# Six gate products beside the banded attention, thirteen beside the sparse one, and the compression's temporaries in two other tiles

## The chip, the cores and the metric

The kernel runs on one NeuronCore of a Trainium2 chip. The metric is the device time of one execution in microseconds (us), from the first instruction to the last; lower is better. The engines are named as the profile names them: PE (TensorE, matrix products), PEld (its weight loads), DVE (VectorE), ACT (ScalarE), POOL (GpSimd) and SP (the queue that issues most transfers). Every engine runs its own list of instructions in order; semaphores tie them together.

## What is computed

The reference is a small model on 512 tokens of width 1024: one block with two feed-forward nets around a mixture of two attentions, then a second block of two layers. All is float32. What the change touches is the attention part of each of these two layers:

```python
g = sigmoid(h @ w_branch_gate)                 # 1024 -> 3 x 1024
o_a = nsa_attention(...)    # sparse: compressed, selected and windowed keys, 8 heads
o_b = swa_sink_attention(...)                  # banded: window of 128, 8 heads
o_c = mla_attention(...)                       # latent: low-rank queries and keys, 8 heads
merged = g_a * (o_a @ w_branch_a) + g_b * (o_b @ w_branch_b) + g_c * (o_c @ w_branch_c)
x = x + merged @ w_out
# inside nsa_attention, for keys and for values:
k_cmp = gelu(blocks(kc) @ w1) @ w2             # the compression
```

## The kernel before, in words

The activations stand with features on the partitions and 512 tokens along the row. A float32 product is made of three products of rounded parts, each part a high and a low piece: high by high, high by low, low by high. A **dense product** of this kind, 128 output features from 1024 inputs, is thus 24 matmuls of 128x512 (lines 143 to 145, `gemm`). Its weights come by a transfer into `wraw` and are taken apart by ACT (line 88, `whi`) and DVE (line 89, `wlo`), one instruction of 128x1024 each per product. A **gate product** is such a product out of `w_branch_gate`; there are 24 in a layer, and each also has a scaling on DVE (line 470), a tanh on ACT (line 471), both on a tile `gt`, and a transfer of `gt` to memory.

In `mix2` the attentions of a layer run one after the other: the banded one (`swa`, four pairs of heads), the sparse one (`nsa`, eight heads), the latent one (`mla`, eight heads). Each is a generator that gives up control after a head (the banded one after each first head of a pair and after each pair). At every such point `pump` lets other generators write a step: queries `qa`, `qb`, keys `kva`, the compression (`inp` prepares its input, `cmp_` has four steps, `end` takes its results), the latents `lt` (four dense products with their normalisation, then a small one), the gates `gts` and the output branches `brs`. A tuple such as `(qa, 1, gts, 1)` says which generators write how many steps. This fixes the order in which the work is written; a scheduler then orders each engine's list by a simulated timeline, and so may draw instructions forward past others that wait, as far as buffers allow.

Two sets of buffers matter for that. In this part all dense products share the two PSUM banks `ps_mm` (`narrow()`): a third product can't start before the first one's result has been taken out. And `mla` begins with four products (lines 1453 to 1455), each worth a quarter of a dense product; their results are taken out by ACT (line 91) and DVE (line 92) into tiles `v`, of which there are four. The compression's inputs (`FL`) hold two of them until it is done; the values of the sparse attention (`VS`) hold the other two until the last sparse head is done.

One sparse head is, on PE: `ps_s` products of keys and queries (line 969, with a mask by line 971), transposes of the probabilities into `ps_t` (995), products with the values into `ps_o` (1002, 1003), and the compressed branch (1280, 1294, 1300), together 98 matmuls, of 8 rows of scores each. Each row goes from PE to DVE (maximum, 973), ACT (exponent, 974), DVE (975, 990), ACT and DVE (halves `ph`, 98 and 99), PE (transposes), ACT (copies `pp`, 997 and 998) and back to PE. In the banded attention the matching lines are 1339 to 1344 (scores), 105 (transposes `ps_t`), 835 (copy `p`) and 1379 (`ps_o`).

The compression keeps two temporaries, `hT` and `s`, in tiles `gt`, of which there are two; the gates use the same two.

Of the kernel before, what the change touches and what calls it, by code (L numbers as in the profile page):

```python
# [844 lines left out]
class Block2(Block1):  # L845
# [205 lines left out]
    def mix2(self, X, U, a, i):  # L1051
# [50 lines left out]
        def queries(out, first):  # L1102
            for c0 in (first, first + 256):
                for ps in proj(c0, 256):
                    out.extend(self.stack_q(self.rope(ps, cosr, sinr), 0.125))
                    yield

        def keys_a():
            for c0 in (768, 1024):
                ka.append(self.stack_k(self.rope(next(proj(c0)), cosr, sinr)))  # L1110
                yield

        def keys_b():
            kb.append(self.stack_k(self.rope(next(proj(1816)), cosr, sinr)))
            yield
            kb.append(self.values_b(next(proj(1944)), R))
            yield

        def gates():
            nonlocal gd  # L1120
            for gd in self.gates(a["w_branch_gate_2"][i], uh, ul, R, 24, f"gates2_{i}"):
                yield

        def branches():
            yield from self.branch(gd[8:16], a["w_branch_b_2"][i], OB, ("uh", "uh"), merged, "ul")
            yield from self.branch(gd[0:8], a["w_branch_a_2"][i], OA, ("uh", "uh"), merged, "ul")


        kvb, kva, qb, qa = keys_b(), keys_a(), queries(QB, 1304), queries(QA, 0)
# [3 lines left out]
        inp, cmp_ = self.compress_in(FL, i, proj, cosr, sinr, R, flat), self.compress(a, i, flat)  # L1133
        gts, brs, lt = gates(), branches(), self.latents(a, i, proj, w_in, uh, ul, R, lat)
        KC = VC = None

        def last():
            nonlocal KC, VC
            KC, VC = next(cmp_)
            yield  # L1140
        end = last()
        plan = ((qb, 1, kva, 1), (inp, 1, qb, 1), (inp, 1, cmp_, 1), (qb, 1, cmp_, 1), (qa, 1, cmp_, 1), (qa, 1, cmp_, 1),
                (qa, 1, end, 1, gts, 1), (kva, 1, qa, 1, gts, 1))
        for n, _ in enumerate(self.swa(QB, *kb, i, OB)):
            self.pump(*plan[n])
        KS, KW = ka


        plan = ((lt, 2), (lt, 2, gts, 1), (lt, 1, gts, 2)) + ((gts, 3),) * 5
        for h, _ in enumerate(self.nsa(QA, KS, KW, KC, VS, VC, G, OA)):  # L1150
            self.pump(*plan[h])
        for h, _ in enumerate(self.mla(lat, a, i, OC)):
# [69 lines left out]
    def compress(self, a, i, flat):  # L1222

        nc = self.nc
        out = []
        for kv in range(2):
            w1 = a["a_cmp_w1_v_2" if kv else "a_cmp_w1_k_2"][i]
            hT, s = self.t("gt"), self.t("gt")
            w2 = a["a_cmp_w2_v_2" if kv else "a_cmp_w2_k_2"][i].rearrange("(k p) n -> p k n", p=128)
            w = hT[:, 128:384].rearrange("p (k n) -> p k n", k=2)  # L1230
            nc.sync.dma_start(w[:, :, 0:64], w2)
            if kv == 0:
                nc.sync.dma_start(w[:, :, 64:128], w2)

            ps = self.bank()
            for half in range(2):
                r = self.raw(8, 256)
                nc.sync.dma_start(r, w1[1024 * half:1024 * half + 1024].rearrange("(k p) n -> p k n", p=128))
                for j in range(8):
                    e = j % 2  # L1240
                    nc.tensor.matmul(ps[64 * e:64 * e + 64, 0:256], flat[kv][:, 8 * half + j].rearrange("p g n -> p (g n)"),
                                     r[:, j], start=half == 0 and j < 2, stop=half == 1 and j > 5)
            nc.scalar.activation(s[0:64, 0:256], ps[64:128, 0:256], AF.Copy)
            nc.vector.tensor_tensor(s[0:64, 0:256], ps[0:64, 0:256], s[0:64, 0:256], op=OP.add)
            yield
            ps = self.bank()
            for m in range(2):
                nc.tensor.transpose(ps[:, 64 * m:64 * m + 64], s[0:64, 128 * m:128 * m + 128], self.ident[0:64, 0:64])
            nc.scalar.activation(hT[:, 0:128], ps[:, 0:128], AF.Gelu_apprx_tanh)
            yield  # L1250
            if kv == 0:
                both = self.t("kc", F32R)
                ps = self.bank()
                for k in range(2):
                    nc.tensor.matmul(ps[:, 0:64], w[:, k], hT[:, 64 * k:64 * k + 64], start=k == 0, stop=k == 1)
                c = both[:, 0:128].rearrange("p (g e n) -> p e g n", g=2, e=2)
                self.split(c[:, 0], c[:, 1], ps[:, 0:64].rearrange("p (g n) -> p g n", g=2))
                out.append([c[:, :, g] for g in range(2)])
            else:
                c = both[:, 128:384]  # L1260
                for g in range(2):
                    ps = self.bank()
                    for k in range(2):
                        nc.tensor.matmul(ps[0:32, 0:64], hT[:, 64 * k + 32 * g:64 * k + 32 * g + 32], w[:, k, 0:64],
                                         start=k == 0, stop=k == 1)
                    o = 128 * g
                    for r in (0, 32):
                        self.split(c[r:r + 32, o:o + 64], c[r:r + 32, o + 64:o + 128], ps[0:32, 0:64], 1 / UP)
                out.append([c[0:64, 0:128], c[0:64, 128:256]])
        yield out  # L1270
# [334 lines left out]
```

## Time and profile before

| | us |
|---|---|
| median of 3 runs | 3258.23 |
| lowest and highest | 3254.02, 3265.27 |
| the profiled execution | 3259.47 |
| its span, first to last instruction | 3257.7 |
| PE busy in the span | 3171.5 (97%) |
| DVE, ACT, POOL busy | 1905.7, 1480.2, 350.7 |
| mean granted clock of PE | 0.985 |

The granted clock is 1.00 at 2.4 GHz and 0.50 at 1.2 GHz; a mean of 0.94 over a stretch says that 12% of it ran at the lower level, and that 6% of its length in PE's work was lost. The banded attention of the first layer lies at about 1265 to 1390 us, the sparse one overlaps its end and goes to 1620, the latent one to 1740; in the second layer they lie some 1005 us later. A matmul's end is modelled in the profile, so PE can show as busy while short waits lie between the starts of its matmuls.

### The profile page before, as it was taken

What the parts mean: (1) busy time and instruction counts of PE and PEld (TensorE: products, weight loads), DVE (VectorE), ACT (ScalarE), POOL (GpSimd) and SP (SyncE); (2) the same over time, 40 slices, a digit from 0 to 9 for tenths busy, and PEclk for the clock granted to TensorE, in tenths of its full rate; (3) what the DMA queues carried; (4) which work ended last, traced back from release to release, by engine and by line L of the source; (5) the groups of instructions that cost most, each with busy time, mean ns of one, the idle gap of its engine ahead of it and who ended that gap; (6) DMA issues with size and microseconds to landing.
All of it is one profiled execution on the core that took longest, in us unless ns stands there. A gap on an engine that the chain in (4) does not pass through costs nothing.

```text
span 3257.7 us, 44744 instructions
## 1 busy us (share of the span) xinstructions
PE 3171.5 (97%) x16695; PEld 2610.2 (80%) x16695; DVE 1905.7 (58%) x3745; ACT 1480.2 (45%) x2929; POOL 350.7 (11%) x562
## 2 busy tenths in 40 slices
PE   8999899999999998999999999999999999999998
PEld 7888888778888887778777888888778878788887
DVE  5344555555744458776677544357876677544355
ACT  4323335644432335667775322234766776322233
POOL 2200231102650020000003000000000002000001
PEclk9999999999999998999999999999989999999999
DMA  5432253336132325423265323224532246332322
GB/s 147 127 104 94 88 172 114 88 118 202 57 120 91 107 70 147 137 79 102 84 188 173 113 92 104 91 91 136 156 90 95 89 141 200 126 104 91 104 84 71
DMA packets 365737, 373.39 MB, mean 115 GB/s; under 512 B 48640, under 2 KB 317824, under 8 KB 365520
## 3 DMA queue, kind: packets, MB, share of 16 engines
q1 hardware_dynamic: 358672, 358.48, 35.5%
q0 software_dynamic: 6640, 12.01, 1.4%
q8 instruction: 131, 2.15, 0.3%
q14 instruction: 86, 0.70, 0.1%
q10 hardware_dynamic: 208, 0.05, 0.0%
HBM read 320.16 MB, written 44.91 MB: 112 GB/s over the span
## 4 chain that ended last, share of the span: by engine, by line
PE 91%; DVE 4%; DMA 2%; ACT 2%; issue 1%; SPq 0%; POOL 0%; DVEq 0%; ACTq 0%; POOLq 0%
PE ps_mm L143 13%; PE ps_mm L144 13%; PE ps_mm L145 13%; PE ps_s L145 6%; PE ps_s L143 6%; PE ps_s L144 6%; PE ps_t L143 6%; PE ps_t L145 6%; PE ps_t L144 6%; PE ps_s L969 3%; PE ps_t L995 2%; PE ps_o L1002 1%; PE ps_o L1003 1%; PE ps_t L105 1%; DMA gt<-gates 1%
## 5 line engine op out<-in xcount | busy, mean ns | idle before, releaser
L88 ACT ACTIVATE whi<-wraw 128x1024 fp32r<-128x1024 f32 (+4 forms) x422 | 414.7, 990 | 823.5 <-PE ps_mm L144 259.7
L143 PE MATMUL ps_mm<-uh,whi 128*128 128x512 f32 (+2 forms) x1648 | 647.0, 393 | 5.0 <-DVE ft L1041 2.8
L145 PE MATMUL ps_mm<-uh,wlo 128*128 128x512 f32 (+2 forms) x1648 | 644.2, 391 | 0.0
L144 PE MATMUL ps_mm<-ul,whi 128*128 128x512 f32 (+2 forms) x1520 | 593.6, 391 | 3.1 <-DVE ul L92 3.1
L89 DVE TENSOR_TENSOR wlo<-wraw,whi 128x1024 fp32r<-128x1024 f32 (+4 forms) x422 | 494.6, 1177 | 161.6 <-ACT whi L88 160.0
L143 PEld LDWEIGHTS ps_mm<-uh,whi 128*128 128x128 f32 (+1 forms) x1648 | 311.7, 189 | 65.9 <-DVE ft L1041 3.2
L145 PEld LDWEIGHTS ps_mm<-uh,wlo 128*128 128x128 f32 (+1 forms) x1648 | 311.0, 189 | 60.4 <-issue 0.2
L144 PEld LDWEIGHTS ps_mm<-ul,whi 128*128 128x128 f32 (+1 forms) x1520 | 287.2, 189 | 57.8 <-DVE ul L92 3.8
L143 PE MATMUL ps_t<-uh,whi 128*128 128x512 f32 (+1 forms) x600 | 231.2, 385 | 0.0
L145 PE MATMUL ps_t<-uh,wlo 128*128 128x512 f32 (+1 forms) x600 | 230.2, 384 | 0.0
L144 PE MATMUL ps_t<-ul,whi 128*128 128x512 f32 (+1 forms) x600 | 230.1, 383 | 0.0
L145 PE MATMUL ps_s<-uh,wlo 128*128 128x512 f32 (+1 forms) x544 | 208.6, 384 | 0.0
L144 PE MATMUL ps_s<-ul,whi 128*128 128x512 f32 (+1 forms) x544 | 208.6, 383 | 0.0
L143 PE MATMUL ps_s<-uh,whi 128*128 128x512 f32 (+1 forms) x544 | 208.4, 383 | 0.0
L88 ACT ACTIVATE dh<-wraw 128x768 fp32r<-128x768 f32 (+2 forms) x102 | 89.9, 898 | 209.1 <-PE ps_mm L144 68.8
L99 DVE SCALAR_TENSOR_TENSOR ph<-p,sa,ph 128x128 f16<-128x128 f32 (+2 forms) x224 | 124.6, 565 | 30.4 <-ACT ph L98 28.4
L89 DVE TENSOR_TENSOR dl<-wraw,dh 128x768 fp32r<-128x768 f32 (+2 forms) x102 | 105.1, 1044 | 62.6 <-ACT dh L88 62.2
L969 PE MATMUL ps_s<-k,q 128*128 128x256 f32 (+1 forms) x448 | 130.7, 383 | 2.4 <-ACT p L974 2.4
L144 PEld LDWEIGHTS ps_t<-ul,whi 128*128 128x128 f32 x600 | 114.8, 191 | 21.3
L143 PEld LDWEIGHTS ps_t<-uh,whi 128*128 128x128 f32 x600 | 114.7, 191 | 21.4
L145 PEld LDWEIGHTS ps_t<-uh,wlo 128*128 128x128 f32 x600 | 114.5, 191 | 21.6
L98 ACT ACTIVATE ph<-p,sa 128x128 f16<-128x128 f32 (+2 forms) x224 | 120.4, 554 | 25.0 <-DVE sa L990 18.7
(655 smaller groups left out, 6417.4 us busy)
## 6 DMA issues: line engine op xcount, KB each, us to landing
wraw<-w_in_in SPq DMA_DIRECT2D x28, 1024.0 KB, 5.4
wraw<-w_branch_gate_in SPq DMA_DIRECT2D x24, 1024.0 KB, 5.7
wraw<-ffn_w_gate_in SPq DMA_DIRECT2D x22, 1024.0 KB, 5.5
wraw<-ffn_w_up_in SPq DMA_DIRECT2D x22, 1024.0 KB, 5.4
wraw<-w_ffn_gate_in SPq DMA_DIRECT2D x22, 1024.0 KB, 5.9
wraw<-w_ffn_up_in SPq DMA_DIRECT2D x22, 1024.0 KB, 5.4
wraw<-ffn_w_down_in SPq DMA_DIRECT2D x24, 768.0 KB, 4.4
gates<-gt SPq DMA_DIRECT2D x64, 256.0 KB, 2.1
```

What stands on the lines that cost most here:

```text
L88: nc.scalar.activation(hi, src, AF.Copy)
L89: nc.vector.tensor_tensor(lo, src, hi.bitcast(F32), op=OP.subtract)
L98: self.nc.scalar.activation(h, P, AF.Copy, scale=scale)
L99: self.nc.vector.scalar_tensor_tensor(l, P, scale, h, op0=OP.mult, op1=OP.subtract)
L105: self.nc.tensor.matmul(out, hl[e][:, cols], self.ident16, start=e == 0, stop=e == 1)
L143: nc.tensor.matmul(o, w[0][k], xh[k][:, cols], start=k == 0, stop=False)
L144: nc.tensor.matmul(o, w[0][k], xl[k][:, cols], start=False, stop=False)
L145: nc.tensor.matmul(o, w[1][k], xh[k][:, cols], start=False, stop=k == kc - 1)
L969: nc.tensor.matmul(ps[:, 0:n], l, r, start=i == 0, stop=i == len(mms) - 1)
L995: nc.tensor.transpose(pt[:, e, k], hl[e][:, k * 128:k * 128 + 128], self.ident16)
L1002: nc.tensor.matmul(o, v, PH[:, k], start=first and k == 0, stop=False)
L1003: nc.tensor.matmul(o, v, PL[:, k], start=False, stop=last and k == nk - 1)
```

## The change

The tuples are altered. Beside the banded attention, `gts` now writes a step at each of the last six points instead of the last two. Beside the sparse one it writes none, none, one, two, three, two, three, two steps after heads 0 to 7, instead of none, one, two and five times three: 13 instead of 18. The rest of the 24 is written beside the latent attention: 5 instead of 4. The compression's `hT` goes from `gt` to a tile `c`, its `s` to a tile `ot`; of each there is one, which the sparse heads use later. No arithmetic is added or taken away.

```diff
         plan = ((qb, 1, kva, 1), (inp, 1, qb, 1), (inp, 1, cmp_, 1), (qb, 1, cmp_, 1), (qa, 1, cmp_, 1), (qa, 1, cmp_, 1),
-                (qa, 1, end, 1, gts, 1), (kva, 1, qa, 1, gts, 1))
+        plan = ((qb, 1, kva, 1), (inp, 1, qb, 1), (inp, 1, cmp_, 1, gts, 1), (qb, 1, cmp_, 1, gts, 1), (qa, 1, cmp_, 1, gts, 1),
+                (qa, 1, cmp_, 1, gts, 1), (qa, 1, end, 1, gts, 1), (kva, 1, qa, 1, gts, 1))
...
-        plan = ((lt, 2), (lt, 2, gts, 1), (lt, 1, gts, 2)) + ((gts, 3),) * 5
+        plan = ((lt, 2), (lt, 2), (lt, 1, gts, 1), (gts, 2), (gts, 3), (gts, 2), (gts, 3), (gts, 2))
...
-            hT, s = self.t("gt"), self.t("gt")
+            hT, s = self.t("c"), self.t("ot")
```

What the scheduler makes of it is seen in the engines' lists. First DVE in the banded attention of the first layer, around the first maximum of the fifth head (line 1348); `wlo` is a product's weights, `gt` the scaled result of a gate product, `rt` and `q` belong to the queries, the rest to the banded heads. Before:

```order
L99 SCALAR_TENSOR_TENSOR ph<-pp,sa,ph 128x128
L1348 TENSOR_REDUCE sa<-ps_s 128x1
L1349 TENSOR_REDUCE sa<-ps_s 128x1
L1358 TENSOR_TENSOR sa<-sa 128x4
L1351 TENSOR_SCALAR sa<-sa,sink 128x2
L1359 RECIPROCAL sa<-sa 128x4
L1360 TENSOR_SCALAR sa<-sa 128x4
```

After, up to the same maximum:

```order
L931 TENSOR_TENSOR rt<-rt,cs 128x512
L470 TENSOR_TENSOR gt<-ps_mm,r 128x512
L932 TENSOR_TENSOR rt<-rt,cs 128x512
L835 COPY p<-ps_t 128x256
L89 TENSOR_TENSOR wlo<-wraw,whi 128x1024
L1348 TENSOR_REDUCE sa<-ps_s 128x1
L1349 TENSOR_REDUCE sa<-ps_s 128x1
```

A gate product's result is now taken out among the banded heads; six stand ahead of the first sparse head's softmax (line 1283) where two stood.

Then ACT in the last sparse head of the first layer, from its compressed branch (`dr`) on; `whi` and `gt` belong to dense products. Before:

```order
L1287 ACTIVATE dr<-dr 128x128
L88 ACTIVATE whi<-wraw 128x1024
L98 ACTIVATE ph<-p,sa 128x512
L471 ACTIVATE gt<-gt 128x512
L974 ACTIVATE p,sa<-ps_s,sa 128x128
L974 ACTIVATE p,sa<-ps_s,sa 128x256
L98 ACTIVATE ph<-p,sa 128x128
L98 ACTIVATE ph<-p,sa 128x256
L88 ACTIVATE c<-ps_t 32x512
L88 ACTIVATE whi<-wraw 128x768
```

After:

```order
L1287 ACTIVATE dr<-dr 128x128
L974 ACTIVATE p,sa<-ps_s,sa 128x256
L98 ACTIVATE ph<-p,sa 128x128
L98 ACTIVATE ph<-p,sa 128x256
L997 ACTIVATE pp<-ps_t 128x4x128
L998 ACTIVATE pp<-ps_t 128x4x128
L974 ACTIVATE p,sa<-ps_s,sa 128x128
L88 ACTIVATE c<-ps_t 32x512
```

No weights and no gates are left in this head's list: they stand ahead of it.

Last PE in the same head, from two products of scores on; `ps_mm` is a dense product. Before:

```order
L969 MATMUL ps_s<-k,q 128x256 x2
L971 LDWEIGHTS identb
L971 MATMUL ps_s<-mask,identb 128x128
L969 MATMUL ps_s<-k,q 128x256
L145 MATMUL ps_mm<-uh,wlo 128x512
L143 MATMUL ps_mm<-uh,whi 128x512
L144 MATMUL ps_mm<-ul,whi 128x512
```

After:

```order
L969 MATMUL ps_s<-k,q 128x256 x2
L971 LDWEIGHTS identb
L971 MATMUL ps_s<-mask,identb 128x128
L969 MATMUL ps_s<-k,q 128x256
L1294 MATMUL ps_t<-ident,dr 32x128 x4
L1002 MATMUL ps_o<-pp,v 128x256
L1003 MATMUL ps_o<-pp,v 128x256
```

The dense matmuls that stood between this head's own are gone from it. Counted over PE's whole list, the longest run of matmuls without a dense one in the attention part is 61 in either layer before, and 163 in the first and 144 in the second after; both hold the whole last sparse head. The four products of lines 1453 to 1455 stand inside that head before, and ahead of the run after, in both layers.

## Rows read from the trace of the kernel before

**Rows 1.** The page: busy time of the engines, and the chain that ended last.
```profile
PE 3171.5 (97%) x16695; PEld 2610.2 (80%) x16695; DVE 1905.7 (58%) x3745; ACT 1480.2 (45%) x2929; POOL 350.7 (11%) x562
PE 91%; DVE 4%; DMA 2%; ACT 2%; issue 1%; SPq 0%; POOL 0%; DVEq 0%; ACTq 0%; POOLq 0%
```

**Rows 2.** Windows: stretch, length, busy us (instructions) per engine, clock, DMA share, GB/s.
```profile
1300.00:1360.00 60.00, 55.91 (x383) 42.63 (x383) 48.59 (x119) 43.41 (x108) 0.42 (x2) 0.94 0.50 153
1395.00:1440.00 45.00, 40.70 (x234) 32.31 (x234) 30.94 (x101) 31.25 (x79) 2.13 (x12) 0.85 0.20 63
1440.00:1600.00 160.00, 160.00 (x972) 128.79 (x971) 109.75 (x279) 111.55 (x273) 7.25 (x42) 1.00 0.29 92
1600.00:1640.00 40.00, 38.11 (x218) 30.14 (x217) 27.30 (x55) 27.99 (x62) 1.73 (x10) 1.00 0.31 90
2310.00:2360.00 50.00, 48.37 (x339) 35.66 (x334) 40.20 (x92) 36.72 (x92) 0.42 (x2) 1.00 0.52 157
2395.00:2450.00 55.00, 50.48 (x289) 40.78 (x288) 35.51 (x116) 35.00 (x91) 2.54 (x14) 0.81 0.17 53
2600.00:2640.00 40.00, 38.10 (x212) 30.41 (x211) 27.83 (x53) 26.89 (x57) 1.54 (x10) 1.00 0.34 96
```

**Rows 3.** Waits of PE, 1300 to 1360 us: us in total, times, longest.
```profile
PE ps_t L105 <- DVE ph L99: 2.8, 3, 1.3
PE ps_o L1379 <- DVE p L835: 0.8, 1, 0.8
```

**Rows 4.** Groups of instructions, 1440 to 1600 us: count, busy us, mean ns, idle before.
```profile
L143 PE MATMUL ps_mm<-uh,whi 128*128 128x512 f32 (+1 forms) x148 | 58.7, 397 | 0.0
...
L974 ACT ACTIVATE p<-ps_s,sa 128x128 f32<-128x128 f32 (+3 forms) x44 | 22.8, 521 | 9.6 <-DVE sa L973 7.9 <-DVE sa L975 1.6
L89 DVE TENSOR_TENSOR wlo<-wraw,whi 128x1024 fp32r<-128x1024 f32 (+1 forms) x18 | 21.7, 1207 | 1.4 <-ACT whi L88 1.2
...
L88 ACT ACTIVATE whi<-wraw 128x1024 fp32r<-128x1024 f32 (+1 forms) x18 | 18.9, 1052 | 7.4 <-PE ps_mm L144 7.4
...
L470 DVE TENSOR_TENSOR gt<-ps_mm,r 128x512 f32<-128x512 f32 x17 | 11.7, 686 | 3.8 <-PE ps_mm L145 3.8
L471 ACT ACTIVATE gt<-gt 128x512 f32<-128x512 f32 x17 | 10.8, 634 | 0.1
```

**Rows 5.** Timeline of PE, two dense matmuls: start us, us, what.
```profile
1281.41 0.39 PE L145 MATMUL ps_mm<-uh,wlo 128*128 128x512 f32 x1
...
1283.45 0.39 PE L145 MATMUL ps_mm<-uh,wlo 128*128 128x512 f32 x1
```

**Rows 6.** Windows: the four stretches of sparse heads without dense matmuls, and their sum.
```profile
1395.20:1405.70 10.50, 7.99 (x59) 5.91 (x58) 9.68 (x33) 9.24 (x25) 0.69 (x4) 0.98 0.03 4
1423.90:1437.90 14.00, 12.21 (x67) 9.58 (x67) 11.07 (x38) 10.94 (x28) 0.75 (x4) 0.69 0.34 113
2395.70:2409.20 13.50, 11.06 (x63) 8.14 (x61) 11.31 (x37) 10.36 (x29) 0.76 (x4) 0.73 0.03 4
2428.10:2442.40 14.30, 12.22 (x66) 9.50 (x66) 12.31 (x39) 11.54 (x30) 0.75 (x4) 0.66 0.33 110
sum 52.30, PE 43.48 PEld 33.13 DVE 44.37 ACT 42.09 POOL 2.95; mean PE 10.87 PEld 8.28 DVE 11.09 ACT 10.52 POOL 0.74
```

**Rows 7.** Timeline of ACT, first and last result `v` in the first layer.
```profile
1606.67 0.68 ACT L91 ACTIVATE v<-ps_mm,rv 128x512 fp32r<-128x512 f32 x1
...
1620.10 0.69 ACT L91 ACTIVATE v<-ps_mm,rv 128x512 fp32r<-128x512 f32 x1
```

**Rows 8.** Timeline of PE at the same place: idle us before, and releaser, in brackets.
```profile
1616.66 0.38 PE L1002 MATMUL ps_o<-pp,v 128*128 128x256 f32 x1 [1.23 <-ACT pp L997]
```

More of the change, by code (lines that the diff above doesn't have):

```diff
@@ L1141, in mix2 @@
         end = last()
-        plan = ((qb, 1, kva, 1), (inp, 1, qb, 1), (inp, 1, cmp_, 1), (qb, 1, cmp_, 1), (qa, 1, cmp_, 1), (qa, 1, cmp_, 1),
-                (qa, 1, end, 1, gts, 1), (kva, 1, qa, 1, gts, 1))
+        plan = ((qb, 1, kva, 1), (inp, 1, qb, 1), (inp, 1, cmp_, 1, gts, 1), (qb, 1, cmp_, 1, gts, 1), (qa, 1, cmp_, 1, gts, 1),
+                (qa, 1, cmp_, 1, gts, 1), (qa, 1, end, 1, gts, 1), (kva, 1, qa, 1, gts, 1))
         for n, _ in enumerate(self.swa(QB, *kb, i, OB)):
```

## The prediction

> **What bounds the kernel now.** I read the page's busy times and chain first. PE is busy for 97% of the span and carries 91% of the chain that ended last [rows 1]. The change adds and removes no matmul, so PE's work stays, and what can move is the time in which PE stands idle or runs at the lower clock. The windows by stage show where that is [rows 2]; there the reader compares PE's busy time with the length, and looks at the clock. Beside the banded attention of the first layer (1300 to 1360 us) PE is idle for 4.1 us and the mean clock is 0.94, which costs another 0.06 x 60 = 3.6 us; in the second layer (2310 to 2360) it is idle for 1.6 us at full clock. In the first sparse heads (1395 to 1440, 2395 to 2450) 4.3 and 4.5 us are idle and the clock costs 0.15 x 45 = 6.8 and 0.19 x 55 = 10.4 us, 26 us together. From 1440 to 1600 us, where sparse heads run with three dense products each, PE is never idle and the clock is 1.00. Last, I looked for what such a head costs without dense products [rows 6].
>
> **A gate product's price.** Nine dense matmuls start within 2.04 us [rows 5], 0.227 us each, so a product is 24 x 0.227 = 5.4 us of PE. It takes 1.2 + 0.7 = 1.9 us of DVE and 1.05 + 0.63 = 1.7 us of ACT [rows 4]. It is PE's filler: while it runs, DVE and ACT can finish the softmax that PE waits for.
>
> **What four more gate products gain beside the banded attention.** The waits named there are PE's transposes behind DVE's halves, and the value product behind a copy on DVE [rows 3]. DVE is busy for 48.6 of 60 us. Four products bring 22 us of work to PE and 7.6 us to DVE, so PE leads DVE by more than before, and the waits should shrink. At most all goes: 4.1 + 3.6 + 1.6 = 9.3 us over both layers. At least nothing goes, if the products stand behind the waits instead of in them. I take 7, since the order has gate results among the banded heads' rows and still keeps stretches of 52 to 66 matmuls without a dense one.
>
> **What the sparse heads lose.** The early heads look alike in the order: two stretches without dense matmuls in each layer, 53 and 61 (then 56 and 61) long before, 51 and 59 (62 and 56) after. I cost them at no change. The last head is another matter. Its own PE list holds 163 (first layer) and 144 matmuls (second) in a row without a dense one, 307 in all, or 307 / 98 = 3.13 heads. The reason lies in the buffers. Of mla's four first products two can be taken out early; the other two need the tiles of `VS`, which the last sparse head still reads. Now all four are issued ahead of that head, the last two hold both `ps_mm` banks through it, and no dense product can start. Before, this jam is short: the first of the four results is taken out at 1606.7 us, the last at 1620.1, and PE's visible wait in it is 1.2 us [rows 7, 8].
>
> Price from below: an unfilled head can't be faster than its busiest engine. From 1440 to 1600 us there are 44 rows of scores, 5.5 heads [rows 4]. ACT's 111.6 us less 18.9 for weights and 10.8 for gates is 81.9, or 14.9 us a head; DVE's 109.75 less 21.7 and 11.7 is 76.4, or 13.9. PE's 160 us less 3 x 148 x 0.227 = 101 is 59, or 10.8 us a head. Unfilled, a head thus loses at least 14.9 - 10.8 = 4.1 us, and 3.13 heads lose 12.8 us.
>
> Price from above: the four unfilled stretches have 255 matmuls in 52.3 us, 0.205 us each [rows 6], where the filled head pays 10.8 / 98 = 0.110. The 307 matmuls would take 62.9 instead of 33.8 us, a loss of 29.1. Those stretches also carry the latents' normalisation on DVE and ACT, which the last head doesn't, but like them it would run partly at the lower clock (0.66 to 0.98 there). I take the middle, 21 us, and keep 12.8 and 29.1 for the range. Of the present end of the sparse attention, idle for 1.9 us in each layer [rows 2], some 2.5 us together is replaced by this, not added to it.
>
> **The other edits.** The compression's temporaries move from `gt` to `c` and `ot`. Their order of reuse is the same (the second pass waits for the first), `c` and `ot` are next used by the first sparse head, after the compression, and the transfers of `w2` on SP wait for the same matmuls as before: nothing, covered by that order; if a gate had to wait for a `gt` instead, it would be one product of 5.4 us. One gate more beside the latent attention, where PE is full: nothing.
>
> **Sum.** 3259.5 (the profiled execution; the median is 1.2 lower) - 7 + 21 - 2.5 = 3271.0 us, of which the price of the unfilled heads alone spans 3262.8 to 3279.1. That is 0.4% slower. About 0.3%, 9.8 us, is what a measurement of this kernel can tell from no change.
>
> **A rule that says otherwise.** Rows 2 show a stretch where DVE is nearly full beside one where PE is. The Trainium skill, Perfetto Trace Analysis, Optimization Strategy, says that where the most contended engine changes over time, interleaving the regimes may improve performance; by that alone the sum would be 3259.5 - 9.3 = 3250 us. The same page says under that heading that bubbles on the engine that should be full can mean that there isn't enough PSUM for the next tile; by that the last head's loss stands, and the sum is mine. The trace bears out the first for 9.3 us in the banded part, and for the second shows only the short jam at 1616.7 us [rows 8]. The first rule's time is a part of the faster rival below and of its chance.
>
> **The rivals.**
> - *Only the engine limit.* The last heads cost the floor of 12.8 us and the banded part gives all 9.3: 3259.5 + 12.8 - 2.5 - 9.3 = 3260.5. For it: in the four stretches ACT is busy for 42.1 of 52.3 us and DVE for 44.4, near their limit, and part of that is the latents'. Against: a row's way from its scores to its values changes engine eight times.
> - *Dearer.* PE falls to the lower clock in the long run and stays there. Then a head takes 21.6 us of PE, more than ACT's 14.9, and 3.13 heads lose 33.8: 3259.5 + 33.8 - 2.5 - 7 = 3283.8. For it: three of the four stretches ran at 0.66 to 0.73 though they are a third as long.
> - *Faster: the filler is free where it was taken.* The last head finishes under PE's own pace because ACT and DVE are rid of the gates, so it costs nothing, and the banded part gives 9.3: 3250.2. If PE then also enters the first sparse heads without a gap and a quarter of their 26 us goes, it is 3259.5 - 9.3 - 6.5 = 3243.7. It decides from the point at which the last heads lose less than 6 us. Against: ACT's 14.9 us a head is above PE's 10.8 without any gate.
> - *The plan changes nothing,* because the scheduler undoes it: 3259.5. The order speaks against it: six gate results stand ahead of the first sparse softmax instead of two.
>
> **How the numbers follow.** My forecast 0.49 (its own times 3263 to 3279), the engine limit 0.22, dearer 0.17, faster 0.10, nothing 0.02. Slower by over 0.3% (above 3268) is the dearer case and 0.40 of the forecast: 0.57. Faster by over 0.3% (below 3248.5) is 0.08 of the faster case. The rest, 0.35, is within 0.3%. For 8 in 10 I leave out the faster case and the upper half of the dearer one: 3255 to 3285.
>
> **What would show it.** In the profile after: in each layer a stretch of some 25 to 35 us at the end of the sparse attention without `ps_mm` matmuls, with ACT and DVE at 80% or more, PE's idle time released by ACT and DVE lines 974 to 998, and a clock below 1.00; no such rows in the middle heads. The first and second `v` results should be taken out well ahead of the third and fourth, a whole head apart. Beside the banded attention idle time and lower clock should fall from 9.3 to 2 us or so. I am wrong if that last stretch loses under 6 us or over 34, if the stretches of the first sparse heads change by more than 5 us in either layer, or if the middle heads, now with two to three gates, show idle time of PE.

## The result and the profile after

The changed kernel takes 3285.61 us (median of 5 runs, 3277.22 to 3290.05), the kernel before 3260.00 in the same comparison (3254.02 to 3265.27). The ratio is 1.0071, with a 95% interval of 1.0047 to 1.0095: slower by 0.7%. The profiled execution of the changed kernel took 3285.61 us itself.

The page, as in [rows 1]:

```profile
PE 3179.7 (97%) x16695; PEld 2614.0 (80%) x16695; DVE 1905.1 (58%) x3745; ACT 1482.4 (45%) x2929; POOL 353.6 (11%) x562
PE 88%; DVE 5%; DMA 3%; ACT 2%; issue 1%; SPq 0%; POOL 0%; DVEq 0%; ACTq 0%; POOLq 0%
```

The engines' work is the same; PE holds 88% instead of 91% of the chain that ended last, and DVE and DMA have a point more each. The windows of the stages, as in [rows 2] (stretch, length, busy us per engine, clock):

```profile
1300.00:1360.00 60.00, 56.36 (x347) 43.55 (x347) 37.64 (x79) 34.52 (x75) 0.21 (x1) 0.97 0.47 145
1440.00:1574.00 134.00, 132.31 (x789) 106.69 (x788) 92.92 (x240) 93.13 (x228) 6.27 (x36) 0.96 0.27 84
1574.00:1617.00 43.00, 38.28 (x263) 29.51 (x261) 33.32 (x97) 38.18 (x104) 3.54 (x20) 0.92 0.24 77
2310.00:2360.00 50.00, 47.81 (x335) 35.61 (x334) 37.62 (x87) 32.41 (x85) 0.19 (x2) 1.00 0.45 135
2590.00:2636.00 46.00, 41.08 (x283) 31.69 (x283) 33.91 (x94) 39.24 (x103) 3.36 (x20) 0.96 0.27 86
```

The banded part is hardly better filled: in the first layer 3.6 us of 60 are idle, where 4.1 were, and in the second 2.2 of 50, where 1.6 were. With the clock of 0.97 (0.03 x 60 = 1.8 us) that is 7.6 us, where the prediction expected 9.3 to fall to about 2. The 1.7 us that are idle between 1440 and 1574 us lie at 1447 and 1448 us, in the second early stretch without dense matmuls and not beside the middle heads. New is the end of the sparse attention: 4.7 and 4.9 us idle and a clock of 0.92 and 0.96. Inside it lie the two long stretches without a `ps_mm` matmul, the counterpart of [rows 6]:

```profile
1588.27:1617.05 28.78, 24.02 (x165) 17.74 (x164) 21.93 (x64) 25.58 (x71) 2.51 (x14) 0.88 0.11 33
2611.42:2635.40 23.98, 19.06 (x145) 13.96 (x144) 17.77 (x51) 21.73 (x59) 2.13 (x12) 0.94 0.03 7
```

They hold 163 and 144 matmuls. At the filled head's 0.110 us each these would take 17.9 and 15.8 us; they took 28.8 and 24.0, so 10.9 + 8.2 = 19.1 us are lost, against 21 in the sum. ACT is busy for 89 and 91% of them, DVE for 76 and 74%, which is less than the 80% that the prediction named. PE's waits there (1574 to 1618 us):

```profile
PE ps_t L995 <- DVE ph L99: 2.5, 5, 1.0
PE ps_s L969 <- ACT p L974: 1.2, 3, 0.6
```

The reason given is in the times at which ACT takes out the four `v` results, as in [rows 7]:

```profile
1579.54 0.69 ACT L91 ACTIVATE v<-ps_mm,rv 128x512 fp32r<-128x512 f32 x1
1583.59 0.68 ACT L91 ACTIVATE v<-ps_mm,rv 128x512 fp32r<-128x512 f32 x1
1615.36 0.76 ACT L91 ACTIVATE v<-ps_mm,rv 128x512 fp32r<-128x512 f32 x1
1620.74 0.69 ACT L91 ACTIVATE v<-ps_mm,rv 128x512 fp32r<-128x512 f32 x1
```

The second and the third are 31.8 us apart, a whole head, and the third and fourth hold both `ps_mm` banks from the fourth product's end, at 1588.4, until 1615.4; the first dense matmul after them starts at 1617.05.

What the sum didn't have is in the banded part and behind the sparse one. PE's longest wait from 1264 to 1400 us in the kernel before:

```profile
PE ps_t L105 <- DVE ph L99: 4.3, 4, 1.4
```

PE's waits in the changed kernel, in the same stretch (two of four) and in a second fence from 1618 to 1792 us (the three longest):

```profile
PE ps_mm L143 <- ACT whi L88: 4.6, 2, 3.5
PE ps_t L105 <- DVE ph L99: 1.4, 1, 1.4
```

```profile
PE ps_s L143 <- ACT oc L88: 2.1, 1, 2.1
PE ps_s L969 <- DMA k<-pe: 1.9, 1, 1.9
PE ps_mm L143 <- DVE rt L1489: 1.2, 1, 1.2
```

In the banded part the wait for DVE's halves has shrunk, and a wait for the weights of dense products has come. From the first product of scores to the second sparse head, PE was idle for 266.80 - 253.40 = 13.4 us before (both layers together) and is for 17.3 now:

```profile
sum 266.80, PE 253.40 PEld 190.06 DVE 212.67 ACT 178.47 POOL 3.85; mean PE 126.70 PEld 95.03 DVE 106.34 ACT 89.23 POOL 1.92
```

```profile
sum 315.40, PE 298.12 PEld 228.52 DVE 228.67 ACT 192.71 POOL 3.50; mean PE 149.06 PEld 114.26 DVE 114.33 ACT 96.36 POOL 1.75
```

The first row is the kernel before, the second the changed one (it is longer, since it holds more gate products).

### The profile page after: what moved, and what is told of

Same layout as the page of the kernel before. It is cut to its first block, busy times and chain, and to the rows that moved or that the text cites. A ratio compares the mean times of both kernels' runs of the same rounds, so it can differ in the third digit from the quotient of the medians.

```text
span 3283.8 us, 44743 instructions
## 1 busy us (share of the span) xinstructions
PE 3179.7 (97%) x16695; PEld 2614.0 (80%) x16695; DVE 1905.1 (58%) x3745; ACT 1482.4 (45%) x2929; POOL 353.6 (11%) x562
## 4 chain that ended last, share of the span: by engine, by line
PE 88%; DVE 5%; DMA 3%; ACT 2%; issue 1%; SPq 0%; POOL 0%; DVEq 0%; ACTq 0%; POOLq 0%
PE ps_mm L143 13%; PE ps_mm L144 13%; PE ps_mm L145 13%; PE ps_s L145 6%; PE ps_t L143 6%; PE ps_s L144 6%; PE ps_s L143 6%; PE ps_t L145 6%; PE ps_t L144 6%; PE ps_s L969 2%; PE ps_t L995 1%; PE ps_o L1002 1%; PE ps_o L1003 1%; PE ps_t L105 1%; DVE x L407 1%
```

## Experiments: the last head

All times below are medians of the runs of a kernel; the kernel before, beside them, had 3258 to 3260 us, and each ratio is to it.

**No jam.** Two of mla's four value products get their result banks from `ps_o` instead of `ps_mm`. Done to the changed kernel:

```diff
         for m in range(4):
...
-            ps = self.bank()
+            ps = self.bank("o") if m > 1 else self.bank()
             for k in range(2):
                 nc.tensor.matmul(ps, kh[k][:, ts], vh[k], start=k == 0, stop=False)
```

> The changed kernel (3285.6 us), but the third and fourth of mla's value products go into the banks ps_o instead of ps_mm, so they no longer hold both ps_mm banks while they wait for the tiles of VS. The list of PE then has no run over 66 matmuls without a dense one, where it had 163 and 144. Theory A (the jam of ps_mm costs the last head of each layer its filler, 10.9 + 8.2 = 19.1 us by the two stretches of the changed kernel): 3266 us, no idle time of PE over 1 us at the end of the sparse attention, the banded part as slow as in the changed kernel. Rival B (the last head is bound by ACT and DVE, and filler put into it only moves the loss): 3280 us or more, with idle time in the same place. Rival C (the ps_o banks are needed by the head itself, so a new jam comes): 3285 us or more, PE waiting at lines 1002 or 1280 to 1300 for a ps_o bank.

Measured: 3261.52 us, ratio 1.0003 (0.9993 to 1.0013). 24.1 us are gone by the medians, and 22 by the two ratios, uncertain by some 8 us. The window in which the changed kernel stood, and the four `v` results:

```profile
1570.00:1620.00 50.00, 50.00 (x313) 40.65 (x312) 38.62 (x99) 39.10 (x94) 2.42 (x14) 1.00 0.33 95
```

```profile
1640.79 0.69 ACT L91 ACTIVATE v<-ps_o,rv 128x512 fp32r<-128x512 f32 x1 [2.85 <-PE ps_o L1003]
1649.38 0.69 ACT L91 ACTIVATE v<-ps_o,rv 128x512 fp32r<-128x512 f32 x1
```

The last two results are now taken out even later than before, and nothing waits for them: PE is never idle in this window and the clock is 1.00. It was the two banks, as theory A says. Rivals B and C are out. The run gave 5 us more than the two stretches hold; in the latent part behind them (1618 us on) the waits fell too, from the rows above to these two:

```profile
PE ps_t L143 <- ACT oc L88: 1.6, 1, 1.6
PE ps_t L145 <- DVE wlo L89: 0.5, 1, 0.5
```

**No jam, old tuples.** The same edit to the kernel before.

> The kernel before with the same edit to mla's value products alone. Theory A: its jam was short (1.9 us idle in each layer at that point), so 3256 to 3260 us, within 0.3% of the kernel before. If the new banks themselves cost something (rival C), slower than 3265 us. The difference to the run of the changed kernel with this edit is what the new tuples and tiles cost apart from the last head: by the stages of the two traces some 8 us beside the banded attention and up to 13 us in the latent one; by the prediction's terms it would be a gain of 7.

Measured: 3255.67 us, ratio 0.9983 (0.9974 to 0.9993). The short jam of the kernel before cost 4.5 us, where the sum had 2.5. And the new tuples, with no jam on either side, cost 3261.5 - 3255.7 = 5.9 us. By the prediction it would be a gain of 7.

**The sparse tuple alone.** The old banded tuple, 13 gates beside the sparse heads, the nine others beside the first two latent heads.

```diff
-        plan = ((lt, 2), (lt, 2, gts, 1), (lt, 1, gts, 2)) + ((gts, 3),) * 5
+        plan = ((lt, 2), (lt, 2), (lt, 1, gts, 1), (gts, 2), (gts, 3), (gts, 2), (gts, 3), (gts, 2))
...
-            self.pump(gts, 2)
+            self.pump(gts, 5 - h)
```

> The kernel before with only the new tuple of the sparse attention (13 gate products); the banded tuple keeps 2, the temporaries stay in gt, and the 9 products left are written after the first two latent heads. PE's list has runs of 142 and 183 matmuls without a dense one at the end of the sparse attention. Theory A: the last heads cost what 325 matmuls at some 0.062 us extra each cost, 20 us, so 3260 + 20 = 3280 us, and the banded part reads as in the kernel before. Rival D (the loss comes from the banded part and its six gates): 3260 to 3265 us.

Measured: 3281.46 us, ratio 1.0054 (1.0042 to 1.0066). The jam comes with the sparse tuple, without any change beside the banded attention. The same with the value products in `ps_o`:

> Old banded tuple with 2 gate products, new sparse tuple with 13, 9 beside the first two latent heads, temporaries in gt, and mla's third and fourth value products in ps_o so that the last head has no jam. It lies between the kernel before with that edit (3255.7) and the changed kernel with it (3261.5), which differ by 5.9 us. Theory A (the four more gates beside the banded attention lose it, by new waits for their weights): 3255 to 3257 us. Rival D (the fewer gates beside the sparse heads, or the more beside the latent ones, lose it): 3260 to 3263 us.

Measured: 3252.87 us, ratio 0.9979 (0.9969 to 0.9988), 2 us under theory A's range; rival D is out. So without the jam, 13 gates beside the sparse heads are as good as 18, and the jam is worth 28.6 us here, for 325 matmuls in the two runs.

**The temporaries.** The changed kernel with `hT` and `s` back in `gt`.

```diff
-            hT, s = self.t("c"), self.t("ot")
+            hT, s = self.t("gt"), self.t("gt")
```

> The changed kernel with the compression's temporaries back in gt; the tuples are the new ones. Theory A (the tiles cost and gain nothing): 3282 to 3289 us. Rival E (the move was needed, because a gate beside the compression would wait for a gt that the compression holds): slower by one gate product or more in each layer, 3296 us or more. Rival F (the single tile c makes the load of w2 wait on SP, and the gate's weights behind it): faster by the 3.5 + 2.7 us that PE stands idle there, 3279 us.

Measured: 3285.91 us, ratio 1.0082 (1.0069 to 1.0096): the changed kernel's time. What the tiles cost or gain can't be told from nothing.

## Experiments: the banded part

The edits below are made to the changed kernel with the value products in `ps_o` (3261.5 us), so that the last head doesn't hide them. PE's long wait in the first layer is at 1339.44 us of the changed kernel. Here is its cause on SP, the queue that loads the weights (start us, us, what):

```profile
1304.36 0.37 SPq L1238 DMA_DIRECT2D wraw<-a_cmp_w_v_in  x1
...
1317.77 0.38 SPq L1238 DMA_DIRECT2D wraw<-a_cmp_w_v_in  x1
...
1328.60 3.66 SPq L930 DMA_DIRECT2D rt<-rt  x4
1332.35 0.53 SPq L1231 DMA_DIRECT2D c<-a_cmp_w_v_in  x1
1333.00 0.42 SPq L133 DMA_DIRECT2D wraw<-w_branch_gate_in  x1
```

and on PE:

```profile
1330.34 3.02 PE L1241 MATMUL ps_mm<-wraw,v 128*64 128x256 f32 x25
...
1339.44 0.79 PE L143 MATMUL ps_mm<-uh,whi 128*128 128x512 f32 x1 [3.54 <-ACT whi L88]
```

Two readings are possible. The gate's weights stand behind rope's transfers and the load of `w2` in SP's order (A1). Or there is no buffer: both `wraw` hold the compression's `w1`, 1 MB each, from 1317.8 us until its products run at 1330.3 (A2). Then the load alone takes 5 us, and nothing else is ready for PE.

**Another queue.** The first three gate transfers go through POOL's queue.

```diff
-    def wgen(self, w, c0, n, k0=0, kc=8, where=None):
+    def wgen(self, w, c0, n, k0=0, kc=8, where=None, q=None):
         r = self.raw(kc, n)
-        self.nc.sync.dma_start(r, w[k0 * 128:(k0 + kc) * 128, c0:c0 + n].rearrange("(k p) n -> p k n", p=128))
+        (q or self.nc.sync).dma_start(r, w[k0 * 128:(k0 + kc) * 128, c0:c0 + n].rearrange("(k p) n -> p k n", p=128))
...
-            for e, p in enumerate(self.wgen(w, c * 128, 256)):
+            for e, p in enumerate(self.wgen(w, c * 128, 256, q=nc.gpsimd if c < 6 else None)):
```

> The changed kernel with the value products in ps_o, and the weights of the first three pairs of gate products loaded from POOL's queue instead of SP's, so that they no longer stand behind the transfers rt<-rt, which wait for ACT, and the load of w2. Theory A1 (the queue order on SP makes the gate's weights late): the waits of PE at line 143 for ACT whi in the banded part, 4.6 us in the first layer and 0.8 in the second, go, and 3 to 6 us with the clock that they cost: 3256 to 3259 us. Rival A2 (the two wraw buffers are what is late: the load can't start earlier from any queue): no change, 3261 us, the same waits for whi. Rival A3 (DVE is the limit there, and the weights' wait only took the place of a wait for DVE): 3260 to 3262 us with waits for DVE ph instead.

Measured: 3269.39 us, ratio 1.0028 (1.0019 to 1.0037): slower than all three expected. The waits for the weights stay, 2.9 us in the first layer and, in the second (2264 to 2400 us), the first row here; the row in the second fence is POOL's own wait, in the first layer:

```profile
PE ps_mm L143 <- ACT whi L88: 6.6, 2, 4.1
```

```profile
POOL wraw L133 <- PE ps_mm L1241: 49.6, 2, 41.0
```

POOL stood idle for 41.0 us at a stretch, until the compression's products freed a buffer. So the order on SP is not what made the first layer's weights late, and A1 is out for it. (In the second layer POOL's wait before this load, 39.5 us, is put down to line 1359 of the banded heads instead.) That the kernel is slower shows in the second layer, where PE is idle for 11.0 of the 136 us from 2264 to 2400, against 4.6 with all loads on SP. There the gate's load from POOL starts at 2347.13 and that of `w_in` from SP at 2347.45, and the gate's lands 8.9 us after its issue, where it took about 6 in the first layer. From SP alone the two had started 1.6 us apart (2342.89 and 2344.47). That the two loads slowed each other is likely by this, but no run isolates it.

**Gates first.** In each banded tuple the gate is written ahead of its neighbours.

```diff
-        plan = ((qb, 1, kva, 1), (inp, 1, qb, 1), (inp, 1, cmp_, 1, gts, 1), (qb, 1, cmp_, 1, gts, 1), (qa, 1, cmp_, 1, gts, 1),
-                (qa, 1, cmp_, 1, gts, 1), (qa, 1, end, 1, gts, 1), (kva, 1, qa, 1, gts, 1))
+        plan = ((qb, 1, kva, 1), (inp, 1, qb, 1), (gts, 1, inp, 1, cmp_, 1), (gts, 1, qb, 1, cmp_, 1), (gts, 1, qa, 1, cmp_, 1),
+                (gts, 1, qa, 1, cmp_, 1), (gts, 1, qa, 1, end, 1), (gts, 1, kva, 1, qa, 1))
```

> As the changed kernel with the value products in ps_o, but in each banded tuple the gate is written before its neighbours, so its weights' load stands ahead of the compression's 1 MB loads and of the rope's transfers. PE's list then has two runs over 46 matmuls without a dense one in the two banded parts, where it has seven. Theory A1 or A2 (weights late, by queue or by buffers): waits for whi go to less than 1 us, 3254 to 3258 us. Rival A3 (DVE is the limit there): 3260 to 3263 us. Rival G (the compression's loads come late instead, and the sparse attention waits for KC at line 1280): slower than 3263 us.

Measured: 3249.35 us, ratio 0.9960 (0.9946 to 0.9975), 5 us under the range of A1 and A2. PE's waits from 1264 to 1400 us name no `whi`:

```profile
PE ps_t L105 <- DVE ph L99: 1.9, 1, 1.9
PE ps_mm L143 <- DVE kc L92: 1.5, 1, 1.5
PE ps_mm L143 <- ACT rt L833: 1.1, 1, 1.1
```

**A place of its own for w1.** The main tiles `x` stand empty between the spill of `x` and the latents; four of them take half of `w1`.

```diff
-                r = self.raw(8, 256)
-                nc.sync.dma_start(r, w1[1024 * half:1024 * half + 1024].rearrange("(k p) n -> p k n", p=128))
+                r = [self.m("x").rearrange("p (k n) -> p k n", k=2) for _ in range(4)]
+                for c in range(4): nc.sync.dma_start(r[c], w1[1024 * half + 256 * c:1024 * half + 256 * c + 256].rearrange("(k p) n -> p k n", p=128))
...
-                                     r[:, j], start=half == 0 and j < 2, stop=half == 1 and j > 5)
+                                     r[j // 2][:, j % 2], start=half == 0 and j < 2, stop=half == 1 and j > 5)
```

> The changed kernel with the value products in ps_o (3261.5 us), and the compression's weights w1 loaded into the main tiles x, which stand empty between the spill of x and the latents, instead of both buffers of wraw; everything else as it was. In the changed kernel both wraw buffers are held by w1 from 1317.8 us until its products (line 1241) at 1330.3 to 1334.7, the gate's load is issued at 1333.0, 0.7 us after the first buffer came free, and PE stands idle for the weights until 1339.4; from POOL's queue the load waited for the same products. Theory A2 (the buffers make the weights late, not the queue): PE's waits for ACT whi in the banded parts (4.6 and 0.8 us) go, and 5 to 12 us with the clock they cost: 3250 to 3257 us. Rival A1 (the queue on SP): waits for whi stay or grow, since w1 now takes four issues for one, 3260 us or more. Rival A3 (DVE or ACT is the limit there): other waits in the same places, 3260 to 3263 us.

Measured: 3245.58 us, ratio 0.9963 (0.9949 to 0.9977): 15.9 us less, more than was expected. No wait for `whi` is left in either banded part, though `w1` now takes four issues on SP for one. The weights' lateness is the buffers' doing, A2. PE's idle time from the first product of scores to the second sparse head falls from 311.00 - 295.96 = 15.0 us (both layers, the changed kernel with the value products in `ps_o`) to 8.1, and the clock gives back some 3 more; where the rest of the 15.9 us lies isn't shown:

```profile
sum 311.00, PE 295.96 PEld 226.72 DVE 228.81 ACT 192.99 POOL 3.51; mean PE 147.98 PEld 113.36 DVE 114.40 ACT 96.50 POOL 1.75
```

Then the same edit to the old tuples, to see whether four gates more are worth something once the weights come in time:

> The old tuples and tiles, with both edits of the last experiment: value products in ps_o and the compression's w1 in the empty tiles x. Measured so far, all with the value products in ps_o: old tuples 3255.7 us, new ones 3261.5, new ones with w1 in x 3245.6. Theory A2 in full (six gate products beside the banded attention do gain what the prediction said, once their weights are in time, and the old tuple has little to gain from w1): 3252 to 3256 us, so that the new tuples are faster by 7 to 10 us on these terms. Rival S (w1 in wraw costs the old tuple the same, and the four gates gain nothing of themselves): 3243 to 3248 us.

Measured: 3244.72 us, ratio 0.9964 (0.9950 to 0.9977). Rival S holds: old and new tuples are equal here, within the some 6 us that the two ratios leave open. PE's idle time in the banded part, as above, old tuples and then new, both with `w1` in `x`:

```profile
sum 259.20, PE 251.04 PEld 188.16 DVE 211.30 ACT 178.61 POOL 3.91; mean PE 125.52 PEld 94.08 DVE 105.65 ACT 89.31 POOL 1.96
```

```profile
sum 299.80, PE 291.70 PEld 223.73 DVE 226.08 ACT 192.25 POOL 3.40; mean PE 145.85 PEld 111.86 DVE 113.04 ACT 96.12 POOL 1.70
```

8.2 and 8.1 us. And the wait that the prediction meant to fill, for DVE's halves, has gone from 4.2 to 1.4 us with the old tuples, with no gate added. The first row is the old tuples with `w1` in `wraw`, the second with `w1` in `x` (PE, 1264 to 1445 us, value products in `ps_o` in both):

```profile
PE ps_t L105 <- DVE ph L99: 4.2, 4, 1.4
```

```profile
PE ps_t L105 <- DVE ph L99: 1.4, 1, 1.4
```

So most of that wait was the softmax seen bare: PE had no dense product whose weights were there.

**Where the rest of the gates stand.** Two more kernels with the value products in `ps_o` put 14 and 12 gates beside the sparse heads instead of 13.

```diff
-        plan = ((lt, 2), (lt, 2), (lt, 1, gts, 1), (gts, 2), (gts, 3), (gts, 2), (gts, 3), (gts, 2))
+        plan = ((lt, 2), (lt, 2), (lt, 1), (gts, 2)) + ((gts, 3),) * 4
```

> The changed kernel with the value products in ps_o and 14 gate products beside the sparse attention (none after the first three heads, then two and four times three) instead of 13, so that 4 stand beside the latent one, as before. The end of the branches, where PE waits 1.6 and 1.1 us for oc in the changed kernel with this edit, tells whether the odd gate there costs it. Theory T (the fifth gate beside the latent heads shifts the branches' work): the 2 to 4 us at the end go, 3258 to 3260 us. Rival U (it doesn't matter how many stand where, as long as no head is without filler): 3261 to 3262 us.

Measured: 3249.03 us, ratio 0.9969 (0.9952 to 0.9985). Neither theory has it; 12 us are more than the whole end of the branches holds. The banded part is the same as with 13 gates, with its hole: PE is idle there for 307.60 - 292.79 = 14.8 us, against 15.0:

```profile
sum 307.60, PE 292.79 PEld 224.63 DVE 226.41 ACT 191.35 POOL 3.44; mean PE 146.40 PEld 112.32 DVE 113.20 ACT 95.67 POOL 1.72
```

Yet the kernel is 6.6 us faster than the old tuples with the same edit (3255.67), where 13 gates were 5.9 us slower. So the 5.9 us can't be put down to the banded part alone.

```diff
-        plan = ((lt, 2), (lt, 2), (lt, 1, gts, 1), (gts, 2), (gts, 3), (gts, 2), (gts, 3), (gts, 2))
+        plan = ((lt, 2), (lt, 2), (lt, 1), (gts, 2), (gts, 3), (gts, 2), (gts, 3), (gts, 2))
```

> The changed kernel with the value products in ps_o, but 12 gate products beside the sparse attention instead of 13 (none after the third head), and so 18 in all ahead of the latent one and 6 beside it. With 14, so 20 ahead and 4 beside, 3249.0 us were measured, with 13 3261.5, though the banded part is the same. A pair of gate products shares one transfer and one wraw buffer; with an odd number ahead of the latent attention half a pair keeps that buffer while mla's own weights need two. Theory P (the odd number is what costs): 3247 to 3253 us. Rival Q (fewer beside the sparse heads is dearer, product by product): 3262 us or more. Rival R (the 12 us between 13 and 14 are the clock's chance and not the plan): 3250 to 3262 us, with the clock telling which.

Measured: 3255.10 us (3245.55 to 3261.86), ratio 0.9987 (0.9974 to 1.0001). Rival Q is out, since it isn't dearer with fewer. The median lies above P's range and inside R's. Against P also speaks the sparse tuple alone with the value products in `ps_o`: it has 2 + 13 = 15 gates ahead of the latent attention, an odd number, and takes 3252.87 us. In part it is the clock: see the last section. At an equal mean clock of 0.986 to 0.987, 13 gates still took 3257.5 to 3259.8 us and 14 took 3249.0 to 3250.4 (12 took 3254.0 to 3261.9). What makes that difference of some 8 us is open. It isn't idle time in the latent part, where T and P look for it: from 1640 to 1790 and 2640 to 2780 us PE is idle for 6.1 us with 13 gates and for 5.6 with 14.

**Together.** Gates first, 14 beside the sparse heads, value products in `ps_o`:

> The two edits that gave a gain together: gates written first in each banded tuple (3249.4 us with 13) and 14 gate products beside the sparse attention (3249.0 with the gates last), value products in ps_o. If the two gains are of different places (the banded part's weights; the latent part), they add: 3237 to 3243 us. If both remove the same loss, 3247 to 3250 us.

Measured: 3240.96 us (3235.21 to 3256.12, 9 runs), ratio 0.9963 (0.9944 to 0.9981). It beats both kernels, as do the two with `w1` in `x`; the intervals of these can't be told apart, and whether the two gains add is thus open.

## Why the prediction came out as it did

The forecast, 3271 us and slower by 0.4%, had the sign, and the measured 3285.6 lies 14.6 us above it: 0.6 above the upper end of the range, and beyond the likeliest case's own 3279. Part of the distance is the comparison's own start: by the ratio of 1.0071, 3259.5 becomes 3282.6, inside the range. The runs split the difference between the kernels, 25.4 us, into the same terms; by the intervals of the ratios, the three measured ones are uncertain by some 3, 5 and 8 us:

| term | forecast, us | measured, us | from |
|---|---|---|---|
| present jam, replaced | -2.5 | -4.5 | 3260.2 to 3255.7 |
| tuples without the last head (with 13 gates beside the sparse ones) | -7 | +5.9 | 3255.7 to 3261.5 |
| last heads unfilled | +21 | +24.1 | 3261.5 to 3285.6 |

- **The last head: right, in place, cause and size.** Both results that wait for `VS` hold both banks, and moving them to `ps_o` gives it all back. The two stretches lose 19.1 us, within the bounds of 12.8 and 29.1, and the waits of the first layer's latent part, which fall from 7.1 to 2.1 us, are as long as the rest of the 24.1; no run isolates them. That 21 came so near is in part luck: it was the middle of two bounds that lie 16 us apart, with no reason of its own. The price came from the four unfilled stretches of the kernel before [rows 6]; the floor from ACT and DVE was too low, since ACT is busy for 90% there and PE still falls to the lower clock for part of it.
- **The failed step: "At least nothing goes, if the products stand behind the waits instead of in them", and the 7 us taken above it.** I read the waits of [rows 3], transposes behind DVE's halves, as a lack of dense products, which is true, and took gate products as the cure, which is not. What lacked was weights: with both `wraw` held by `w1`, no further product could be made ready, whichever it was. The four more products need two more transfers through the same two buffers, and with them the wait for `ph` turned into one for `whi`; PE's idle time in the banded part rose from 13.4 to 17.3 us instead of falling. With the weights in time and 13 gates beside the sparse heads the four gates gain nothing that the runs can tell, 3245.6 against 3244.7 us. The bound from below should have allowed a loss. How large this term is stays open: it was +5.9 us with 13 gates, and with 14 it would be -6.6, though the banded part is the same. The hole and its cause are shown; that it makes up the 5.9 us is not. No run has `w1` in `x` and 14 gates together. SP's timeline of the kernel before would have shown the hole, and the prediction didn't read it. From 1308.66 to 1325.11 us no load into `wraw` starts:

```profile
1308.66 0.37 SPq L1238 DMA_DIRECT2D wraw<-a_cmp_w_v_in  x1
...
1325.11 0.53 SPq L133 DMA_DIRECT2D wraw<-w_in_in  x1
```

- **The early sparse heads: right.** In the first layer the two stretches (from 1413.33 and from 1443.72 us) take 11.4 and 13.0 us, in the second (from 2437.51 and from 2460.50) 9.5 and 14.4, against 10.5, 14.0, 13.5 and 14.3 [rows 6]: no layer changes by more than 5 us. The middle heads show no idle time.
- **The temporaries: right** (3285.9 against 3285.6 us). **One gate more beside the latent attention: too low.** Nothing was put down, and PE's waits in the first layer's latent part come to 7.1 us, of which 2.1 stay without the jam. No run isolates those.
- **The rivals.** "Only the engine limit" and "faster" fell with the jam's price and with the banded part, which gave none of its 9.3 us; "the plan changes nothing" fell with the time. "Dearer" gave 3283.8, close to the time, but for a cause that isn't there: PE's clock in the two stretches is 0.88 and 0.94, not 0.50.
- The Trainium skill, Perfetto Trace Analysis, Optimization Strategy, has both rules that were weighed. It says that consistent bubbles on the engine that should be saturated can mean that there isn't enough SBUF or PSUM for the next tile. Moving the value products to `ps_o` bears that out for PSUM, with 24.1 us, and moving `w1` out of `wraw` bears it out for SBUF, with the waits for `whi` gone. The prediction weighed PSUM alone. That interleaving regimes may improve performance isn't borne out with 13 gates beside the sparse heads: 5.9 us were lost while the filler's weights had no buffer, and nothing was gained once they had one.

## What to carry to other kernels

Before adding filler to a stretch, ask why the filler that is there doesn't run: see when its weights' loads were issued, and who holds their buffers. A product whose result must wait for another stage's tile should not stand in the banks that everything else shares; banks from elsewhere for two results were worth 24.1 us in the changed kernel and 4.5 in the kernel before. A term that was measured beside one neighbouring order needn't hold beside another: a single gate more beside the sparse heads turned the sign of one here. And when work is taken from a stretch, count the longest run in each engine's list that is left without it, and price it by a like run of the trace.

## What the runs showed of the hardware

The same PE list took different times, nearly all of it by the granted clock. From the first banded product of scores to the fourth sparse head of the first layer, the kernels with 13, 14 and 12 gates (value products in `ps_o`; the rows stand in this order) have the same 1241 matmuls in the same order:

```profile
1266.80:1491.50 224.70, 212.36 (x1243) 165.05 (x1242) 159.93 (x381) 139.31 (x324) 4.44 (x26) 0.95 0.39 116
```

```profile
1265.70:1485.30 219.60, 207.86 (x1242) 161.68 (x1240) 159.35 (x381) 138.81 (x324) 4.37 (x26) 0.97 0.39 118
```

```profile
1272.00:1492.80 220.80, 208.07 (x1243) 161.86 (x1241) 159.43 (x381) 138.99 (x324) 4.37 (x26) 0.97 0.39 117
```

They differ by 4 to 5 us in 220, at clocks of 0.95 and 0.97; PE's idle time, 12.3, 11.7 and 12.7 us, differs by 1.0. Over a whole execution the kernel with 12 gates ran from 3245.55 us at a mean clock of 0.990 to 3261.86 at 0.986. A difference of a few us between two profiles of this kernel is therefore read from idle time and from the waits first, and from the clock only over many runs.
